# x^T of the second attention 32 bytes further on in its SBUF tile

## The chip, the cores and the metric

The kernel runs on one core of a Trainium2 chip. The metric is the device time of one execution in microseconds (us), as the median of several runs. Engines are named as in the profile: PE (TensorE; PEld is its weight load), DVE (VectorE), ACT (ScalarE), POOL (GpSimd), SP (SyncE, which issues the DMAs).

## What is computed

A decoder trunk of two layers on 256 tokens of 1024 features in float32. Each layer is a mixer and a SwiGLU FFN with RMS norms ahead of both, and a last norm follows. The first mixer is a dilated sliding-window attention with three patterns, the second is forgetting attention. Cut to what matters:

```
h = x
h = h + dilated_mixer(rmsnorm(h, a_norm), a_w_in, a_w_out)
h = h + swiglu(rmsnorm(h, ffn_norm[0]), ffn_w_gu[0], ffn_w_down[0])
h = h + forgetting_mixer(rmsnorm(h, b_norm), b_w_in, b_f, b_w_out)
h = h + swiglu(rmsnorm(h, ffn_norm[1]), ffn_w_gu[1], ffn_w_down[1])
return rmsnorm(h, final_norm)

def forgetting_mixer(h, w_in, b_f, w_out):      # the second attention
    proj = h @ w_in                              # q, k, v of 16 heads, and 16 gates
    log_f = log_sigmoid(gates + b_f); c = cumsum(log_f)
    s = q k^T / 8 + c_i - c_j, causal; p = softmax(s)
    return (p v) @ w_out
```

## The kernel before

There are four stages that read normalised activations as x^T: the first attention, the first FFN, the second attention and the second FFN. In each, x^T lies in one tile "xt" of 128 partitions x 8 (blocks of 128 features) x 2 (high and low part) x 256 tokens, of type fp32r, 16384 bytes per partition. The tag has one buffer, so all four stages use the same addresses. The weights come by DMA in pieces of 128 x 1024 ("raw") and are split by ACT into a high part "wh" and by DVE into a low part "wl" (`piece`, `split`, lines 73 and 75), four buffers of 8192 bytes each.

A product with x^T is three matmuls (`mm3`, lines 178 and 183): high x high, high x low, low x high. It comes in two forms:

- feature products (`proj_feat`): a 128 x 128 block of the weights is stationary, 256 tokens of x^T move, and the result is feature-major. Eight of the second attention's twelve units are of this form (queries and keys of four quads of heads), with 2 x 8 x 3 = 48 matmuls in a unit. The gates and up-projections of the FFNs are of it too.
- token products (`proj_tok`, `proj_pair`): a 128 x 128 block of x^T is stationary and 256 or 512 columns of weights move. The values are made by them, and the first three units of each FFN.

In the profile's rows the moving operand stands first: `ps_mm<-xt,wh` is a feature product, `ps_mm<-wh,xt` a token product. Each matmul has a weight load of its own on PEld, which runs while the matmul before it moves its columns.

Where things lie: the pool "ap" gives each tag a place in the order of first use, in the order h, ot (high and low), gap, xt, xn (the buffers of sums, sqs, junk and xn), rs_a, v, rt, fm0 and so on. The tile "gap" of 112 floats is never read or written; it moves xt. In the built program the weights start at 25952 + n x 8192 bytes, which is 352 modulo 512, and xt at 145184, which is 288 modulo 512: 64 bytes in front of the weights. Blocks of x^T and of the weights follow each other by multiples of 512 bytes, so this holds for every operand of these products, but for those that take every second token. The products of the FFN's way down (`ps_o<-wh,al` and the like) have both operands at 352 modulo 512.

What sets the order around the change: PE runs its matmuls in the order of the code. In the second attention three value units come first, the first two of them together, with the norm of the second 128 tokens (`norm_t`: DVE line 166, PE line 171) between; then the gates (`gates_1`, line 786; `softplus`, the transpose at line 799 and a chain of small steps on DVE and POOL, lines 805 to 818), then the eight feature units and the last value unit. `gates_2` (transposes at 824, a scan at 828, copies at 830) writes the last rows of the key operand "z"; ACT's line 914 writes its other rows. The scores (line 844) of a quad are put between the halves of later feature units, the transposes of the probabilities (275) and the products with v (286) after them. The first scores stand after the first half of the third feature unit.

Line 395 makes "rs_a" with four columns for the first attention's factors of the norm, line 543 "rt" with two columns for the same factors in another order of tokens.

Of the kernel before, what the change touches and what calls it, by code (L numbers as in the profile page):

```python
# [10 lines left out]
F32 = mybir.dt.float32  # L11
F32R = mybir.dt.float32r
AF = mybir.ActivationFunctionType
ALU = mybir.AluOpType
AX = mybir.AxisListType

P = 128
D = 1024
S = 256
KT = D // P  # L20
# [11 lines left out]
def trunk(ctx: ExitStack, tc: tile.TileContext, T, out):  # L32
    nc = tc.nc
# [3 lines left out]
    ap = ctx.enter_context(tc.tile_pool(name="ap", bufs=1))  # L37
# [4 lines left out]
    def first():  # L42

        return tc.high_priority(offset=300)

    def psum(tag):
        return ps.tile([P, 512], F32, tag=tag, name=f"ps_{tag}", bufs=2)
# [15 lines left out]
    mhalf = cst.tile([P, 1], F32, name="mhalf")  # L63
# [30 lines left out]
    def fm_tile(tag, n, bufs):  # L94
        return tuple(ap.tile([P, n, S], F32R, tag=f"{tag}{x}", name=f"{tag}{x}", bufs=bufs) for x in "hl")
# [1 line left out]
    class XT(tuple):  # L97
        pass

    def xt_tile():  # L100
        full = ap.tile([P, KT, 2, S], F32R, tag="xt", name="xt", bufs=1)
        x = XT((full[:, :, 0, :], full[:, :, 1, :]))
        x.full = full
        return x
# [24 lines left out]
    def weights(nm, i, after=None):  # L129

        upto = order.index((nm, i)) + AHEAD
        while state["next"] <= min(upto, len(order) - 1):
            key = order[state["next"]]
            cuts = []
            ready[key] = piece(key, cuts)
            for cut in cuts:
                cut(after)
            state["next"] += 1
        return ready.pop((nm, i))
# [46 lines left out]
    def both(pair, *idx):  # L186
        return tuple(x[idx] for x in pair)


    def early(x, b):  # L190

        x = x.rearrange("p (n b) -> p b n", b=2)
        return x if b is None else x[:, b]
# [58 lines left out]
    def values_12(v, os):  # L252

        for a in range(2):
            v[1 + a] = v_tile()
        with first():
            for t in range(2):
                for a in range(2):
                    rows = slice(a * 64, a * 64 + 64)
                    for g in range(2):  # L260
                        nc.scalar.activation(v[1 + a][g * 64:g * 64 + 64, t * S:(t + 1) * S],
                                             os[t][rows, g * S:(g + 1) * S], AF.Copy, scale=r_a[t][rows])
# [41 lines left out]
    for i, c in enumerate(room):  # L304
        b = 1 + (i > 1)
        n = S + 512
# [12 lines left out]
        for j in range(b):  # L319
            xk.append(both_k[:, j, :S])  # L320
            wk.append(both_k[:, j, S:])

    ap.tile([P, 112], F32, tag="gap", name="gap", bufs=1)
    xt = xt_tile()

    r_a = []
    lead = [psum("sc") for _ in range(2)]
# [62 lines left out]
    def rstd_a():  # L390

        o = psum("tr")
        for t in range(2):
            nc.tensor.matmul(o[:, t:t + 1], part[0][:, t * P:(t + 1) * P], one, start=True, stop=True)
        v = ap.tile([P, 4], F32, tag="rs_a", name="rs_a", bufs=1)
        with first():
            nc.scalar.activation(v[:, :2], o[:, :2], AF.Copy, bias=EPS)
            nc.gpsimd.tensor_tensor(v[:, 2:], v[:, :2], mhalf.to_broadcast([P, 2]), op=ALU.pow)
        r_a.extend(v[:, 2 + t:3 + t] for t in range(2))

    x = []

    ot = fm_tile("ot", KT, 1)
# [99 lines left out]
    for i, (hq, g, w) in enumerate(a_units):  # L503
# [19 lines left out]
        if w < 2:  # L523
# [4 lines left out]
            if i == 2:  # L528
                values_12(quad["v"], lead)

                wt = weights("a_in", 1)
                o_next = psum("mm")
                rb = psum("tr")

                def rows():
                    for t in range(2):
                        nc.tensor.matmul(rb[:, t * P:(t + 1) * P], r_a[t].to_broadcast([P, P]), ident,
                                         start=True, stop=True)

                proj_feat(xt, wt, o_next[:, :S], 0, (6, rows))  # L540
                for c in (rcos, rsin):
                    nc.vector.tensor_tensor(c, c, rb[:, :S], op=ALU.mult)
                rt = ap.tile([P, 2], F32, tag="rt", name="rt", bufs=1)
                tmp = ap.tile([P, D], F32, tag="xn", name="rd", bufs=2)[:, :S].rearrange("p (b c) -> p b c", b=2)
                e = early(rb[:, :S], None)
                nc.vector.tensor_tensor(tmp, e, ident[:, None, :].to_broadcast([P, 2, P]), op=ALU.mult)
                nc.vector.tensor_reduce(rt, tmp, axis=AX.X, op=ALU.add)
# [63 lines left out]
                parts.append(sq(hn[:, s]))  # L611
        return hn, parts

    def out_proj(nm, ot, h, grow, done, banks):

        ws = [weights(nm, i) for i in range(4)]
        xt = xt_tile()
        res = []

        def part(t, acc, nk):  # L620
            last = None
            for n, k in nk:
                c = (k % 2) * D + n * 512
                last = mm3(acc[n], both(ot, ALL, k, slice(t * P, (t + 1) * P)),
                           both(ws[k // 2], ALL, slice(c, c + 512)), k == 0, k == KT - 1)
            return last

        def cols(ks):
            return [(n, k) for n in range(2) for k in ks]

        for t in range(2):
            acc = [psum(banks[t]) for _ in range(2)]
            if t == 0:

                nk = cols(range(done))
                last = part(t, acc, nk[:done])
                nk = nk[done:]
                for i in sorted(due):
                    with tc.issue_after(last.ins):
                        for fn, a in due[i]:  # L640
                            fn(*a)
                    last = part(t, acc, nk[:2]) or last
                    nk = nk[2:]
                due.clear()
                part(t, acc, nk)
                last = part(t, acc, cols(range(done, KT)))
            else:
                part(t, acc, cols(range(2)))
                with tc.issue_after(last.ins):
                    part(t, acc, cols(range(2, 6)))  # L650
                    norm_t(*res[0], grow, xt, 0)
                    part(t, acc, cols(range(6, KT)))
            res.append(residual(acc, h[t], f"h_{nm}{t}"))
        return res, xt
# [93 lines left out]
        return res  # L748

    g_f = load_grow(1)  # L750
    hs, xt = out_proj("a_out", ot, x, g_f, 6, ("sc", "mm"))
    maskb = const("maskb", [P, 3 * P])
    sel = const("sel", [80, NH])
    bf = const("bf", [NH, 1])
    wf32 = const("b_f_in", [P, KT * NH])
    nxt = {}

    def mid(h0):
        nxt["g"] = load_grow(2)
        nxt["xt"] = xt_tile()  # L760
        norm_t(*h0, nxt["g"], nxt["xt"], 0)

    hs = ffn(0, hs, xt, g_f, mid)
    xt, g_b = nxt["xt"], nxt["g"]

# [66 lines left out]
    ot = fm_tile("ot", KT, 1)  # L832
# [99 lines left out]
        for fn, a in due.pop(i, ()):  # L932
            fn(*a)
    g_f = load_grow(3)
    hs, xt = out_proj("b_out", ot, [h for h, _ in hs], g_f, 5, ("mm", "sc"))

    def finish(t, h, parts):
        r = rstd(parts)
# [10 lines left out]
    hs = ffn(1, hs, xt, g_f, mid)  # L949
# [4 lines left out]
    for o, (a, b) in zip(acc, ((0, 512), (512, 256), (768, 256))):  # L954
        s = slice(a, a + b)
# [8 lines left out]
    v = ap.tile([P, 2], F32, tag="rs", name="rs", bufs=4)  # L964
# [99 lines left out]
```

## Time and profile before

| what | us |
|---|---|
| median of 3 runs | 761.44 (761.38 to 761.49) |
| the profiled execution's own time | 761.3 |
| its span, first to last instruction | 759.4 |
| PE busy in the span | 749.7 |
| DVE busy | 511.1 |
| ACT busy | 402.7 |
| POOL busy | 32.4 |

The granted clock of TensorE is 0.997 of full speed over the span. A matmul's duration in the profile is longer than the time from its start to the next one's, since matmuls are pipelined. The distance between starts is what a row of matmuls costs; the mean duration moves with it where nothing is waited for.

### The profile page before, as it was taken

What the parts mean: (1) busy time and instruction counts of PE and PEld (TensorE: products, weight loads), DVE (VectorE), ACT (ScalarE), POOL (GpSimd) and SP (SyncE); (2) the same over time, 40 slices, a digit from 0 to 9 for tenths busy, and PEclk for the clock granted to TensorE, in tenths of its full rate; (3) what the DMA queues carried; (4) which work ended last, traced back from release to release, by engine and by line L of the source; (5) the groups of instructions that cost most, each with busy time, mean ns of one, the idle gap of its engine ahead of it and who ended that gap; (6) DMA issues with size and microseconds to landing.
All of it is one profiled execution on the core that took longest, in us unless ns stands there. A gap on an engine that the chain in (4) does not pass through costs nothing.

```text
span 759.4 us, 14132 instructions
## 1 busy us (share of the span) xinstructions
PE 749.7 (99%) x5810; PEld 695.6 (92%) x5810; DVE 511.1 (67%) x758; ACT 402.7 (53%) x664; POOL 32.4 (4%) x51
## 2 busy tenths in 40 slices
PE   8999999999999999999999999999999999999996
PEld 7999999999998799999999988999889999999995
DVE  6899987986988476555556374888756655556533
ACT  7737539448538455534445354587645434455521
POOL 1110000010010000000000003100000000000000
PEclk9999999999999999999999999999999999999998
DMA  8855553653555367556567444634426665566601
GB/s 329 281 189 192 168 184 105 211 183 104 188 187 177 95 215 243 195 193 195 186 207 239 147 164 142 220 115 142 135 76 228 224 196 193 186 203 202 216 1 55
DMA packets 38352, 135.01 MB, mean 178 GB/s; under 512 B 4368, under 2 KB 5648, under 8 KB 38288
## 3 DMA queue, kind: packets, MB, share of 16 engines
q1 hardware_dynamic: 38144, 134.01, 53.3%
q8 instruction: 45, 0.74, 0.4%
q14 instruction: 19, 0.16, 0.1%
q10 hardware_dynamic: 144, 0.10, 0.0%
HBM read 133.05 MB, written 1.05 MB: 177 GB/s over the span
## 4 chain that ended last, share of the span: by engine, by line
PE 93%; ACT 2%; issue 2%; DMA 1%; DVE 1%; SPq 0%; POOL 0%; POOLq 0%; ACTq 0%; DVEq 0%
PE ps_mm L183 32%; PE ps_mm L178 17%; PE ps_tr L183 9%; PE ps_sc L183 9%; PE ps_o L183 7%; PE ps_tr L178 5%; PE ps_sc L178 4%; PE ps_o L178 3%; PE ps_tr L275 2%; PE ps_o L286 2%; PE ps_sc L844 1%; DMA otl<-in_lead 1%; ACT wh L73 1%; PE ps_tr L171 1%; PE ps_sc L441 1%
## 5 line engine op out<-in xcount | busy, mean ns | idle before, releaser
L73 ACT ACTIVATE wh<-raw 128x1024 fp32r<-128x1024 f32 x236 | 244.0, 1056 | 220.0 <-PE ps_tr L183 67.3
L75 DVE TENSOR_TENSOR wl<-raw,wh 128x1024 fp32r<-128x1024 f32 x236 | 284.6, 1222 | 99.1 <-ACT wh L73 98.7
L178 PE MATMUL ps_mm<-xt,wh 128*128 128x256 f32 x816 | 227.2, 279 | 0.0
L183 PE MATMUL ps_mm<-xt,wl 128*128 128x256 f32 x816 | 225.8, 277 | 0.1
L183 PE MATMUL ps_mm<-xt,wh 128*128 128x256 f32 x816 | 225.7, 277 | 0.0
L178 PEld LDWEIGHTS ps_mm<-xt,wh 128*128 128x128 f32 x816 | 153.3, 188 | 0.6 <-issue 0.3
L183 PEld LDWEIGHTS ps_mm<-xt,wl 128*128 128x128 f32 x816 | 153.3, 188 | 0.5 <-DVE wl L75 0.5
L183 PEld LDWEIGHTS ps_mm<-xt,wh 128*128 128x128 f32 x816 | 153.4, 188 | 0.1
L183 PE MATMUL ps_tr<-xt,wh 128*128 128x256 f32 x304 | 83.8, 276 | 0.0
L183 PE MATMUL ps_tr<-xt,wl 128*128 128x256 f32 x304 | 83.8, 276 | 0.0
L178 PE MATMUL ps_tr<-xt,wh 128*128 128x256 f32 x304 | 83.6, 276 | 0.0
L685 DVE TENSOR_TENSOR sa<-ps_tr,sa 128x256 f32<-128x256 f32 x38 | 16.1, 424 | 73.6 <-PE ps_tr L183 73.6
L183 PEld LDWEIGHTS ps_tr<-xt,wh 128*128 128x128 f32 x304 | 57.1, 188 | 0.0
L183 PEld LDWEIGHTS ps_tr<-xt,wl 128*128 128x128 f32 x304 | 57.1, 188 | 0.0
L178 PEld LDWEIGHTS ps_tr<-xt,wh 128*128 128x128 f32 x304 | 56.9, 188 | 0.0
L178 PE MATMUL ps_mm<-wh,xt 128*128 128x256 f32 (+1 forms) x160 | 53.1, 332 | 0.0
L183 PE MATMUL ps_mm<-wl,xt 128*128 128x256 f32 (+1 forms) x164 | 52.2, 322 | 0.0
L183 PE MATMUL ps_mm<-wh,xt 128*128 128x256 f32 (+1 forms) x164 | 52.1, 321 | 0.0
L183 PEld LDWEIGHTS ps_mm<-wl,xt 128*128 128x128 f32 x164 | 31.1, 190 | 2.6
L183 PEld LDWEIGHTS ps_mm<-wh,xt 128*128 128x128 f32 x164 | 30.8, 190 | 2.8 <-DVE xt L75 0.3
L178 PEld LDWEIGHTS ps_mm<-wh,xt 128*128 128x128 f32 x160 | 30.4, 190 | 3.0
L183 PE MATMUL ps_sc<-wh,al 128*128 128x512 f32 (+1 forms) x82 | 31.4, 387 | 0.0
(237 smaller groups left out, 1170.3 us busy)
## 6 DMA issues: line engine op xcount, KB each, us to landing
raw<-in_gu SPq DMA_DIRECT2D x88, 512.0 KB, 4.7
raw<-in_a_in SPq DMA_DIRECT2D x68, 512.0 KB, 4.3
raw<-in_dn SPq DMA_DIRECT2D x44, 512.0 KB, 4.7
raw<-in_b_in SPq DMA_DIRECT2D x24, 512.0 KB, 4.8
raw<-in_a_out SPq DMA_DIRECT2D x8, 512.0 KB, 5.3
raw<-in_b_out SPq DMA_DIRECT2D x8, 512.0 KB, 3.9
grow<-in_norms SPq DMA_DIRECT2D x4, 512.0 KB, 6.1
x<-in_x SPq DMA_DIRECT2D x2, 512.0 KB, 5.4
```

The costliest lines, as they stand in the source:

```text
L73: a = nc.scalar.activation(view(hi), src, AF.Copy)
L75: return a, nc.vector.tensor_tensor(view(lo), src, view(hi).bitcast(F32), op=ALU.subtract)
L171: nc.tensor.transpose(tr[:, k * P:(k + 1) * P], xn[:, kk * P:(kk + 1) * P], ident)
L178: nc.tensor.matmul(o, sh, mh, start=start, stop=False)
L183: last = nc.tensor.matmul(o[:, u], s, m[:, u], start=False, stop=end and u.stop == n)
L275: nc.tensor.transpose(tr[:, i * P:(i + 1) * P], b, ident)
L286: nc.tensor.matmul(o[h * HD:(h + 1) * HD], v[:, c:c + HD], w(h), start=start, stop=stop)
L441: nc.tensor.matmul(sc[h][a * 64:a * 64 + 64, o:o + 64], q[hr[h], b // 2, c], k[hr[h], b // 2, c], start=True, stop=True)
L685: nc.vector.tensor_tensor(a, u, sg, op=ALU.mult)
L844: last = nc.tensor.matmul(scs[h][:, qb * P:qb * P + (qb + 1) * P], qz[h][rows[h], pr, qb * P:(qb + 1) * P], kz[h][rows[h], pr, :(qb + 1) * ...
```

## The change

`xt_tile` gets an argument "front", the distance in bytes at which x^T lies in front of the weights modulo 512. The tile is made 120 floats longer than x^T, and x^T starts 128 - front/4 floats into it. The first attention and both FFNs ask for 64, the second attention for 32. The tile "gap" goes, and the two columns of "rt" become columns 4 and 5 of "rs_a", which grows from four to eight.

In the built program the tile starts at 144736, where "gap" was. x^T of three stages stays at 145184. That of the second attention is at 145216, which is 320 modulo 512. The tiles between xt and rt (the two xn buffers, rs_a, the seven v buffers) lie 32 bytes higher than before, v at 352 instead of 320 modulo 512. From fm0 on every tile has its old address, and so has everything in front of xt. The instructions of every engine, their order and their waits are the same as before.

```diff
-    def xt_tile():
-        full = ap.tile([P, KT, 2, S], F32R, tag="xt", name="xt", bufs=1)
+    def xt_tile(front):
+        n = KT * 2 * S
+        at = 128 - front // 4
+        tile = ap.tile([P, n + 120], F32R, tag="xt", name="xt", bufs=1)[:, at:at + n]
+        full = tile.rearrange("p (k x s) -> p k x s", k=KT, x=2)
         x = XT((full[:, :, 0, :], full[:, :, 1, :]))
...
-    ap.tile([P, 112], F32, tag="gap", name="gap", bufs=1)
-    xt = xt_tile()
+    xt = xt_tile(64)
...
-        v = ap.tile([P, 4], F32, tag="rs_a", name="rs_a", bufs=1)
+        v = ap.tile([P, 8], F32, tag="rs_a", name="rs_a", bufs=1)
...
+        r_a.append(v[:, 4:6])
...
-                rt = ap.tile([P, 2], F32, tag="rt", name="rt", bufs=1)
+                rt = r_a.pop()
...
-    def out_proj(nm, ot, h, grow, done, banks):
+    def out_proj(nm, ot, h, grow, done, banks, front):
...
-        xt = xt_tile()
+        xt = xt_tile(front)
...
-        nxt["xt"] = xt_tile()
+        nxt["xt"] = xt_tile(32)
```

Both calls of `out_proj`, which make the x^T of the two FFNs, pass 64.

## Rows read from the trace of the kernel before

**Rows 1.** The profile page: the span, the engines' busy time, and the chain that ended last by engine.
```profile
span 759.4 us, 14132 instructions
...
PE 749.7 (99%) x5810; PEld 695.6 (92%) x5810; DVE 511.1 (67%) x758; ACT 402.7 (53%) x664; POOL 32.4 (4%) x51
...
PE 93%; ACT 2%; issue 2%; DMA 1%; DVE 1%; SPq 0%; POOL 0%; POOLq 0%; ACTq 0%; DVEq 0%
```

**Rows 2.** Windows: stretch in us, its length, busy time (and instructions) of each engine, granted clock, DMA share, GB/s. First attention, then the second attention in two stretches of feature units.
```profile
14.00:240.00 226.00, 225.89 (x2041) 213.65 (x2040) 198.87 (x304) 134.23 (x221) 11.16 (x17) 1.00 0.56 185
...
472.10:498.00 25.90, 25.66 (x212) 25.21 (x211) 19.15 (x44) 17.32 (x36) 4.54 (x3) 1.00 0.48 164
498.00:532.20 34.20, 34.20 (x287) 31.41 (x286) 28.31 (x58) 25.62 (x62) 2.51 (x4) 1.00 0.46 146
```

**Rows 3.** Timeline of PE (start in us, duration in us, what): the first matmul of a feature unit and that of the next one, in the first attention and in the second.
```profile
29.55 0.28 PE L178 MATMUL ps_mm<-xt,wh 128*128 128x256 f32 x1
...
34.99 0.28 PE L178 MATMUL ps_mm<-xt,wh 128*128 128x256 f32 x1
...
472.11 0.28 PE L178 MATMUL ps_mm<-xt,wh 128*128 128x256 f32 x1
...
477.76 0.28 PE L178 MATMUL ps_mm<-xt,wh 128*128 128x256 f32 x1
```

**Rows 4.** Groups of PE's instructions by line and shape from 14 to 240 us (first attention), feature products: count, busy us, mean ns of one, idle before.
```profile
L183 PE MATMUL ps_mm<-xt,wl 128*128 128x256 f32 x384 | 106.3, 277 | 0.1
L183 PE MATMUL ps_mm<-xt,wh 128*128 128x256 f32 x384 | 106.1, 276 | 0.0
```

**Rows 5.** The same from 472 to 498 us (second attention).
```profile
L183 PE MATMUL ps_mm<-xt,wl 128*128 128x256 f32 x64 | 18.0, 281 | 0.0
L183 PE MATMUL ps_mm<-xt,wh 128*128 128x256 f32 x64 | 18.0, 281 | 0.0
```

**Rows 6.** The same from 498 to 543 us (second attention; 192 feature products up to 532 us).
```profile
L183 PE MATMUL ps_mm<-xt,wh 128*128 128x256 f32 x65 | 18.0, 277 | 0.0
L183 PE MATMUL ps_mm<-xt,wl 128*128 128x256 f32 x65 | 18.0, 276 | 0.0
```

**Rows 7.** The same from 262 to 450 us (first FFN): feature products, then products of the way down with both operands at the same place modulo 512, of 512 and of 256 columns.
```profile
L183 PE MATMUL ps_tr<-xt,wl 128*128 128x256 f32 x152 | 41.9, 276 | 0.0
...
L183 PE MATMUL ps_o<-wl,ah 128*128 128x512 f32 x30 | 11.7, 389 | 0.0
...
L183 PE MATMUL ps_o<-wh,al 128*128 128x256 f32 x16 | 3.2, 283 | 0.0
...
L183 PE MATMUL ps_o<-wl,ah 128*128 128x256 f32 x16 | 3.2, 280 | 0.0
```

**Rows 8.** The same from 450 to 472 us (second attention), token products of 512 and 256 columns. L178's mean holds the first one after a transpose.
```profile
L183 PE MATMUL ps_mm<-wh,xt 128*128 128x512 f32 x15 | 6.0, 400 | 0.0
L183 PE MATMUL ps_mm<-wl,xt 128*128 128x512 f32 x15 | 5.9, 395 | 0.0
...
L183 PE MATMUL ps_sc<-wh,xt 128*128 128x256 f32 x16 | 4.5, 280 | 0.0
L183 PE MATMUL ps_sc<-wl,xt 128*128 128x256 f32 x16 | 4.5, 279 | 0.0
```

**Rows 9.** The chain that ended last, from 482 to 488 us: start, us, what.
```profile
486.62 0.24 issue
486.86 1.33 PE ps_sc L844 x7
```

**Rows 10.** Timeline of DVE around the gates, 469 to 487 us; in brackets the idle time before and what ended it.
```profile
469.29 0.19 DVE L805 COPY gates<-ps_tr 128x32 f32<-128x32 f32 x1 [0.26 <-PE ps_tr L799]
...
475.46 0.18 DVE L810 TENSOR_SCALAR gates<-gates 128x32 f32<-128x32 f32 x1 [5.54 <-POOL gates L809]
...
482.70 2.36 DVE L75 TENSOR_TENSOR wl<-raw,wh 128x1024 fp32r<-128x1024 f32 x2
484.98 0.67 DVE L828 TENSOR_TENSOR_SCAN v<-v,ps_tr 16x256 f32<-16x256 f32 x1
485.69 0.86 DVE L830 COPY z<-v 16x512 f32<-16x512 f32 x2
```

**Rows 11.** Timeline of ACT at the same place.
```profile
485.08 1.06 ACT L73 ACTIVATE wh<-raw 128x1024 fp32r<-128x1024 f32 x1 [2.50 <-DVE wl L75]
486.17 1.21 ACT L914 ACTIVATE z<-ps_mm 64x512 f32<-64x512 f32 x2
```

**Rows 12.** Timeline of PE from 498.6 us: the first feature products after transposes.
```profile
498.82 0.28 PE L183 MATMUL ps_mm<-xt,wh 128*128 128x256 f32 x1
498.94 0.28 PE L183 MATMUL ps_mm<-xt,wl 128*128 128x256 f32 x1
499.06 0.28 PE L178 MATMUL ps_mm<-xt,wh 128*128 128x256 f32 x1
499.17 0.28 PE L183 MATMUL ps_mm<-xt,wh 128*128 128x256 f32 x1
499.29 0.28 PE L183 MATMUL ps_mm<-xt,wl 128*128 128x256 f32 x1
```

**Rows 13.** Timeline of DVE at the second norm, and at the weight split ahead of the gates' sums.
```profile
457.37 1.42 DVE L166 SCALAR_TENSOR_TENSOR xn<-hf,rs,grow 128x512 f32<-128x512 f32 x2 [0.46 <-POOL rs L151]
...
465.56 2.36 DVE L75 TENSOR_TENSOR wl<-raw,wh 128x1024 fp32r<-128x1024 f32 x2 [4.60 <-ACT wh L73]
```

**Rows 14.** Groups of PE's instructions from 14 to 240 us: products of the probabilities with v, 64 columns.
```profile
L286 PE MATMUL ps_o<-pt,v 128*64 128x64 f32 x96 | 3.8, 221 | 0.0
```

More of the change, by code (lines that the diff above doesn't have):

```diff
@@ L394, in rstd_a @@
             nc.tensor.matmul(o[:, t:t + 1], part[0][:, t * P:(t + 1) * P], one, start=True, stop=True)
-        v = ap.tile([P, 4], F32, tag="rs_a", name="rs_a", bufs=1)
+        v = ap.tile([P, 8], F32, tag="rs_a", name="rs_a", bufs=1)
         with first():
             nc.scalar.activation(v[:, :2], o[:, :2], AF.Copy, bias=EPS)
-            nc.gpsimd.tensor_tensor(v[:, 2:], v[:, :2], mhalf.to_broadcast([P, 2]), op=ALU.pow)
+            nc.gpsimd.tensor_tensor(v[:, 2:4], v[:, :2], mhalf.to_broadcast([P, 2]), op=ALU.pow)
         r_a.extend(v[:, 2 + t:3 + t] for t in range(2))
+        r_a.append(v[:, 4:6])
     x = []
@@ L750, in trunk @@
     g_f = load_grow(1)
-    hs, xt = out_proj("a_out", ot, x, g_f, 6, ("sc", "mm"))
+    hs, xt = out_proj("a_out", ot, x, g_f, 6, ("sc", "mm"), 64)
     maskb = const("maskb", [P, 3 * P])
@@ L934, in trunk @@
     g_f = load_grow(3)
-    hs, xt = out_proj("b_out", ot, [h for h, _ in hs], g_f, 5, ("mm", "sc"))
+    hs, xt = out_proj("b_out", ot, [h for h, _ in hs], g_f, 5, ("mm", "sc"), 64)
     def finish(t, h, parts):
```

## Prediction

> **What bounds the kernel now.** The page comes first: PE is busy for 749.7 of the 759.4 us of the span, and the chain that ended last is PE for 93% [rows 1]. The windows by stage then say that PE has no gap worth the name in the stages concerned, and that the granted clock is 1.00 in all of them [rows 2]. So a time is won or lost here by how fast PE goes through its matmuls, unless PE is made to wait for something that another engine delivers at a time of its own.
>
> What is to be seen next is that matmuls of one shape don't all go at one pace. I take the pace from starts in the timeline: in the first attention 48 feature products (x^T moving, 256 columns) start at 29.55 and the next 48 at 34.99 us, which is 5.44 / 48 = 113.3 ns each; in the second attention 48 of the same take from 472.11 to 477.76 us, 5.65 / 48 = 117.7 ns [rows 3]. The mean duration of one tells the same in whole nanoseconds, 276 against 281, and is quicker to read over long stretches: 276 for the first attention [rows 4], 281 for the second from 472 to 498 us [rows 5], 276 again for it from 498 to 532 us [rows 6], 276 in the first FFN [rows 7]. So before the change one half of the second attention's feature products goes at the long pace, the other half at the short one, at the very same addresses.
>
> Other relative addresses have paces too. Where x^T is stationary (64 bytes in front of the moving weights) a 256-column product takes 279 or 280 ns [rows 8]. Where both operands are at the same place modulo 512 (the halved products of the FFN's way down) it takes 280 and 283 [rows 7]. 276 is the least and 283 the most that a settled 256-column product shows, so these two are my bounds for any product with x^T at the new place.
>
> **The change part by part.** No instruction is added, taken away or moved, and no wait or semaphore differs; the code moves addresses alone. There are three parts.
>
> 1. x^T of the second attention, 64 to 32 bytes in front of the weights. The products that read it: 8 feature units of 48, so 384 (192 of them at the long pace, 192 at the short one); 96 token products of 256 columns with x^T stationary; some 50 token products of 512 columns; 8 for the gates.
>
> *Feature products, long half (472 to 498 us).* If the new place settles them at the short pace they win 192 x (117.7 - 113.3) = 0.85 us of PE work; if at the worst that a row shows they lose 192 x 2 ns (281 to 283) = 0.38 us. But not all of this is on the path. The chain shows PE stopped for 0.24 us in front of the first scores at 486.86 us [rows 9]. What it waits for is no matmul. Scores need the operand z. Its last pieces are DVE's copies from 485.69 us (0.86 us) and ScalarE's at 486.17 us, which stand behind a weight split that waited 2.50 us for DVE [rows 10, 11]. DVE works without a break since 475.46 us, and there it had idled 5.54 us for a POOL instruction that follows the gates' transpose at 469 us [rows 10]. So from the gates' transpose on there is a chain over POOL, DVE and ScalarE whose length doesn't depend on PE's pace. The 48 + 48 + 24 = 120 feature products ahead of the first scores would win 0.53 us and hand all of it back as a longer wait: 0.24 + 0.53 = 0.77 us. What stays are the 24 + 48 = 72 products from 488 to 498 us: 72 x 4.4 = 0.32 us. After 488 us PE waits for nothing in this stage: 0.24 us is all the idle time of its first half, and the second has none [rows 2]. So these 0.32 us go through to the end, past the output projection and the FFN, where PE is just as full. On the losing side the wait is a cover of 0.24 us and then gone.
>
> *Feature products, short half (498 to 532 us).* Nothing to win. Bounds: 0, and 192 x 7 ns (276 to 283) = 1.34 us lost. I take 0: they enter from transposes and settle within a few steps (the starts from 498.82 to 499.06 us lie 0.12 us apart, the next one 0.11 [rows 12]; over all of them the means are 277 and 276 [rows 6]), so the short pace is one they are drawn to, and 32 bytes are half of the distance to the place where 283 is seen.
>
> *Token products (x^T stationary).* At 280 now; bounds 276 and 283, so from -4 to +3 ns each. 24 of the 96 are at 469 to 472 us, inside the stretch that the gates' chain covers. The others are 18 that follow the norm's transposes at 459.32 us, the 6 ahead of them, and 48 of the last value unit at 532 to 543 us. 72 x (-4 to +3) is -0.29 to +0.22 us. I take 0, since the new distance (32) lies between one with 280 (64) and one with 280 and 283 (0).
>
> *Wide token products.* 395 and 400 ns [rows 8] against 389 at equal places [rows 7]: at best 50 x 8 = 0.4 us. More than half stands ahead of 457.37 us, where the second norm on DVE sets the time of the transposes [rows 13], or beside the weight split that DVE begins at 465.56 us and that the gates' sums are queued behind [rows 13]; I count 0.1 us at most on the path, and take 0.
>
> 2. The tiles behind x^T (xn with its users, rs_a, v) lie 32 bytes higher. v is the stationary operand of the products with the probabilities: 64-column ones take 221 ns in the first attention [rows 14], and they come in pairs that overlap. 256 of them in all; 1 ns each way is 0.26 us, and I take 0. They could alter the pace at which the next feature products settle, see the rivals.
>
> 3. rt is now a piece of rs_a. Same writer, same readers, same waits: 0.
>
> The sum is -0.32 us on the profiled execution, whose own time is 761.3 us (span 759.4), 0.14 under the median of 761.44. I apply it to the median: 761.1 us.
>
> What speaks against a change of any size is a rule of the Trainium skill, TensorE: Matmul & The Clock Gate, Part 2, step by step: PE has two independent read ports, one for the moving operand and one for the weight load, so loading the next weights takes no bandwidth from the running matmul. By it the place of one operand against the other could not matter and the sum would be 0 (761.4). The trace bears it out in part only: it has 276, 280 and 283 ns for one shape at different places, which the rule has no cause for, but it also has 276 and 281 at one and the same place.
>
> **The rivals.**
> *The place does nothing; how PE enters decides.* For it: the long half is entered from token products at 280 and then from scores, the short half from transposes, and the addresses are the same in both [rows 5, 6]. Against it: the token products stand at 279 and 280 in all three of their rows, though some of them follow transposes and others wide products [rows 8]. Then the 72 products stay at 117.7 and the time is 761.4.
>
> *The long pace everywhere.* At 32 bytes the short pace is no longer settled on and the other 192 feature products go at 281 too: 192 x 4.4 = +0.85 us, 762.3 us. For it: the long pace exists at 64 already, and stays for 48 products and more in a row. Still within the bound of no change.
>
> *The pace of equal places, the slower side.* 32 bytes may be near enough to 0 that the 283 ns of [rows 7] hold. Short half +1.34; the 72 exposed ones of the long half 72 x 2 = +0.14; token products +0.22; the 144 covered steps 120 x 2 + 24 x 3 = 0.31, less the cover of 0.24, +0.07. That is +1.77 us, 763.2 us. It decides from 113.3 + 4 ns in the short half on, since 0.2% (what a measurement of this kernel can tell from no change) is 1.52 us and the short half brings most of it.
>
> *The tiles moved along.* v or xn at a new place lets feature units elsewhere settle otherwise. A unit of 48 that goes from the short pace to the long one costs 48 x 4.4 = 0.21 us, and one that settles wrongly can hand its pace on to the next. Four units: +0.85 us beside the -0.32, so 762.0 us. Hardly any gain is to be had there, as the rows already say 276 [rows 4].
>
> **How the numbers follow.** Forecast (long half to the short pace, 120 steps of it lost to the gates' chain): 761.1 us, 0.43. No effect: 761.4, 0.24. Long pace everywhere: 762.3, 0.14. Pace of equal places: 763.2, 0.11. Tiles moved along: 762.0, 0.08. The low end is the forecast with token and wide products at their best, 761.12 - 0.29 - 0.1 = 760.7, less 0.2 us for what entries may bring: 760.5. The high end takes in the long pace everywhere with token products at their worst, 762.3 + 0.22, so 762.6; the pace of equal places is left out. Faster than 759.92 is reached by no case, 0.02 for what I have not seen; slower than 762.96 by most of the pace of equal places, 0.09; 0.89 in between.
>
> **What would show it.** In the profile after: the feature products of 472 to 498 us at 276 ns instead of 281, those of 498 to 532 us still at 276; PE's stop in front of the first scores (L844, a line that moves by four) grown from 0.24 to about 0.8 us; token products of the second attention near 280; all rows of the other stages as they were. The forecast is wrong if the stop stays at 0.24 us while the products are faster (then the chain over DVE is no anchor and 0.5 us more are won), if 281 or more stands at 498 to 532 us, or if the first attention's or an FFN's groups change at all.

## The result and the profile after

| what | before | after |
|---|---|---|
| median of 5 runs, us | 761.49 (761.38 to 762.82) | 764.41 (764.01 to 765.19) |
| ratio | | 1.0041, 95% interval 1.0030 to 1.0051 |
| the profiled execution's own time, us | 761.3 | 765.19 |
| its span, us | 759.4 | 763.2 |

The change makes the kernel 2.9 us (0.4%) slower. The forecast was 761.1 us and its range ended at 762.6. The profiled execution of after is the slowest of its five runs, so its 3.8 us of longer span are some 0.9 us more than the medians differ by.

The page of after answers to [rows 1]. The whole difference of the spans is PE's: 753.5 - 749.7 = 3.8 us more busy time with the same 5810 matmuls, and the chain that ended last is as much PE's as before.

```profile
span 763.2 us, 14132 instructions
...
PE 753.5 (99%) x5810; PEld 699.2 (92%) x5810; DVE 510.4 (67%) x758; ACT 402.1 (53%) x664; POOL 32.9 (4%) x51
...
PE 93%; ACT 2%; issue 2%; DMA 1%; DVE 1%; SPq 0%; POOL 0%; POOLq 0%; ACTq 0%; DVEq 0%
```

Where along the span does it arise? The timeline of PE at the places of [rows 3] (start in us, duration, what) tells it by subtraction.

```profile
29.87 0.28 PE L183 MATMUL ps_mm<-xt,wh 128*128 128x256 f32 x1
...
35.52 0.28 PE L183 MATMUL ps_mm<-xt,wh 128*128 128x256 f32 x1
...
474.80 0.28 PE L183 MATMUL ps_mm<-xt,wh 128*128 128x256 f32 x1
...
480.48 0.28 PE L183 MATMUL ps_mm<-xt,wh 128*128 128x256 f32 x1
```

At the unit that began at 29.55 us before, after is 0.32 us late; at the first feature unit of the second attention (472.11 before) it is 2.69 us late. The first products that read the moved x^T are token products, ahead of that unit: they start at 451.90 us before and at 454.54 us after, so after is 2.64 us late there already. So 2.32 of the 3.8 us are lost between 29.55 us and any product that reads the moved x^T. The unit at 29.87 us takes 5.65 / 48 = 117.7 ns a product, where it took 113.3. The rest, 3.8 - 2.69 = 1.1 us, is lost behind 472 us.

The groups by stage put names to it. First attention (14 to 240 us), to be held against [rows 4]: the feature products went from 277 and 276 to 279.

```profile
L188 PE MATMUL ps_mm<-xt,wl 128*128 128x256 f32 x384 | 107.2, 279 | 0.1
L188 PE MATMUL ps_mm<-xt,wh 128*128 128x256 f32 x384 | 107.0, 279 | 0.0
```

A mean of 279 is not one pace, but a mixture. The same view of after from 30 to 46 us, a stretch of feature products alone, has 281:

```profile
L188 PE MATMUL ps_mm<-xt,wl 128*128 128x256 f32 x46 | 12.9, 281 | 0.0
L183 PE MATMUL ps_mm<-xt,wh 128*128 128x256 f32 x46 | 12.9, 281 | 0.0
```

and the windows say the same without durations. They are given for three stretches, first of before, then of after (columns as in [rows 2]): PE has no gap in any, the granted clock is 1.00 in all, and after gets 138 matmuls into 16 us where before got 144, 214 where it got 225, 213 where it got 227.

```profile
30.00:46.00 16.00, 16.00 (x144) 16.00 (x143) 15.65 (x26) 9.43 (x12) 0.00 (x0) 1.00 0.64 217
...
119.00:143.00 24.00, 24.00 (x225) 23.66 (x224) 19.13 (x32) 19.56 (x37) 0.00 (x0) 1.00 0.39 128
...
179.00:205.00 26.00, 26.00 (x227) 25.88 (x226) 20.24 (x31) 18.78 (x26) 0.00 (x0) 1.00 0.44 142
```

```profile
30.00:46.00 16.00, 16.00 (x138) 16.00 (x137) 14.90 (x24) 9.52 (x12) 0.00 (x0) 1.00 0.61 202
...
119.00:143.00 24.00, 24.00 (x214) 23.50 (x213) 19.17 (x33) 20.42 (x39) 0.00 (x0) 1.00 0.36 118
...
179.00:205.00 26.00, 26.00 (x213) 25.55 (x212) 19.77 (x32) 19.08 (x30) 0.00 (x0) 1.00 0.45 143
```

The first FFN (262 to 450 us, answering to [rows 7]) is as it was:

```profile
L188 PE MATMUL ps_tr<-xt,wl 128*128 128x256 f32 x152 | 41.9, 276 | 0.0
```

Second attention, 472 to 498 us (answering to [rows 5]) and 498 to 543 us (to [rows 6]): the long half stayed at 281, the short half went from 277 and 276 to 281.

```profile
L188 PE MATMUL ps_mm<-xt,wh 128*128 128x256 f32 x56 | 15.7, 281 | 0.0
L188 PE MATMUL ps_mm<-xt,wl 128*128 128x256 f32 x56 | 15.7, 281 | 0.0
```

```profile
L188 PE MATMUL ps_mm<-xt,wl 128*128 128x256 f32 x73 | 20.5, 281 | 0.0
L188 PE MATMUL ps_mm<-xt,wh 128*128 128x256 f32 x73 | 20.5, 281 | 0.0
```

PE's stop in front of the first scores (chain that ended last, answering to [rows 9]) is 0.36 us, not the 0.8 that was forecast: the products ahead of it did not become faster.

```profile
489.37 0.36 issue
489.73 1.33 PE ps_sc L848 x7
```

### The profile page after: what moved, and what is told of

Read it like the earlier page. It is cut to its first block, busy times and chain, and to the rows that moved or that the text cites. A ratio compares the mean times of both kernels' runs of the same rounds, so it can differ in the third digit from the quotient of the medians.

```text
span 763.2 us, 14132 instructions
## 1 busy us (share of the span) xinstructions
PE 753.5 (99%) x5810; PEld 699.2 (92%) x5810; DVE 510.4 (67%) x758; ACT 402.1 (53%) x664; POOL 32.9 (4%) x51
## 4 chain that ended last, share of the span: by engine, by line
PE 93%; ACT 2%; issue 2%; DMA 1%; DVE 1%; SPq 0%; POOL 0%; POOLq 0%; ACTq 0%; DVEq 0%
PE ps_mm L188 33%; PE ps_mm L183 17%; PE ps_tr L188 9%; PE ps_sc L188 9%; PE ps_o L188 7%; PE ps_tr L183 5%; PE ps_sc L183 4%; PE ps_o L183 3%; PE ps_tr L280 2%; PE ps_o L291 2%; PE ps_sc L848 1%; DMA otl<-in_lead 1%; ACT wh L73 1%; PE ps_tr L176 1%; PE ps_sc L445 1%
## 5 line engine op out<-in xcount | busy, mean ns | idle before, releaser
L183 PE MATMUL ps_sc<-wh,ah 128*128 128x512 f32 x80 | 31.4, 392 | 0.0
```

The source lines that it names most:

```text
L183: nc.tensor.matmul(o, sh, mh, start=start, stop=False)
```

## The experiments

Two numbers go through this section. Both are counted from the starts in PE's timeline of one profiled execution of each kernel: how many feature products were followed by the next matmul after 115.5 to 125 ns (called long; the short pace is 113.3), and by how much the steps of all feature products of a stage exceed 113.33 ns (called excess; steps over 125 ns hold a change of shape or a wait and are left out). Before has 66 long ones of 1152 in the first attention (excess 0.37 us) and 197 of 384 in the second (0.90 us); after has 591 (2.71 us) and 356 (1.84 us). The two FFNs have some 25 long ones of 912 each (0.18 us) in every kernel but the two that move their x^T.

The theories that the expectations name: **A**, two causes: the tiles moved along (v, xn) change the pace on which stretches of the first attention settle, and x^T at 32 has no short pace. **B**, chance: a stretch settles on either pace from one execution to the next, whatever the addresses. **C**, the moved tiles make the whole loss. **D**, what counts of v is its place against the tile "pt" that moves over it in the products with the probabilities. **E**, what counts of v is its place against the operands of the feature products that follow.

**The parts of the change, one by one.** First the moved tiles without x^T at 32: after, with one number altered.

```diff
-        nxt["xt"] = xt_tile(32)
+        nxt["xt"] = xt_tile(64)
```

> x^T of the second attention back at 64 bytes; xn, rs_a and v stay 32 bytes higher, as after the change. Theory A (two causes: the new place of x^T costs about 1.1 us in the second attention, the tiles moved along cost the first attention what is left): about 763.3 us, feature products of the second attention from its second half on at 276 ns again, stretches of the first attention at 281. Theory B (the place of x^T is the one cause, the first attention goes at the long pace by chance in some executions of any version): the median of before, 761.5 us, with single executions up to 2 us above. Theory C (the moved tiles alone make the whole loss, in both attentions): 764.4 us.

Measured: 764.05 us (763.62 to 764.2) against 761.11 (760.04 to 762.69) for before on the same chip, ratio 1.0039 (1.0025 to 1.0053). Long products: 602 in the first attention, 83 in the second. Groups from 14 to 240 us:

```profile
L183 PE MATMUL ps_mm<-xt,wh 128*128 128x256 f32 x384 | 107.6, 280 | 0.0
L188 PE MATMUL ps_mm<-xt,wl 128*128 128x256 f32 x384 | 107.2, 279 | 0.1
```

So the loss in the first attention comes from the tiles alone, and it is most of what the whole change costs. By its time alone this kernel lies nearer to theory C's 764.4 us than to A's 763.3; what tells them apart are the groups, the next kernel and the repeats further down. The second attention did in part what the prediction had hoped to get from x^T at 32: the 120 products ahead of the first scores went short but for 5, though x^T did not move, while of the 72 behind the scores 70 stayed long. And the stop in front of the first scores grew to 0.73 us:

```profile
489.07 0.46 PE L848 MATMUL ps_sc<-z,z 80*128 80x128 f32 x2 [0.73 <-ACT z L918]
```

Then the reverse: x^T of the second attention at 32, and every tile behind it 512 bytes on, so that their places modulo 512 stay. Three small tiles of the second attention share the buffers of the first one's for the room.

```diff
-        full = ap.tile([P, KT, 2, S], F32R, tag="xt", name="xt", bufs=1)
+        n = KT * 2 * S
+        tile = ap.tile([P, n + 128], F32R, tag="xt", name="xt", bufs=1)[:, at:at + n]
...
-        nxt["xt"] = xt_tile()
+        nxt["xt"] = xt_tile(8)
...
-        nm = stat_tile("nm_b", 4)
+        nm = stat_tile("nm", 4)
```

> Only x^T of the second attention is 32 bytes in front of the weights; every other tile keeps its old place modulo 512 (those behind x^T lie 512 bytes higher, and the second attention's small statistics share the first one's buffers). Theory A: about 762.6 us, all feature products of the second attention at 281 ns or so, the first attention at 276. Theory B: 764.4 us or, in executions without the chance, 762.6. Theory C: 761.5 us.

Measured: 761.82 us (761.26 to 762.71), ratio 1.0011 (1.0002 to 1.0019). The first attention has 63 long products, as before; the second 354 of 384. Groups from 498 to 543 us:

```profile
L185 PE MATMUL ps_mm<-xt,wl 128*128 128x256 f32 x64 | 18.0, 281 | 0.0
L185 PE MATMUL ps_mm<-xt,wh 128*128 128x256 f32 x64 | 18.0, 281 | 0.0
```

In front of the first scores PE no longer stops at all (the product ahead starts at 485.99, the scores at 486.27 us). x^T at 32 is a loss by itself, of 0.7 us (A had put it at 1.1), and it doesn't touch the first attention.

**Which of the moved tiles.** v alone, 32 bytes on behind a pad; then xn alone, by placing rs_a ahead of it.

```diff
-        v = ap.tile([P, 4], F32, tag="rs_a", name="rs_a", bufs=1)
+        v = ap.tile([P, 8], F32, tag="rs_a", name="rs_a", bufs=1)
+        ap.tile([P, 8], F32, tag="pad", name="pad", bufs=1)
...
-                rt = ap.tile([P, 2], F32, tag="rt", name="rt", bufs=1)
+                rt = r_a.pop()
```

> Only v is 32 bytes higher than before (352 modulo 512); x^T, xn and rs_a are at their old places. If v is what the first attention's loss hangs on (its products with the probabilities stand right in front of feature units that changed pace), 762.5 to 763.5 us with stretches of the first attention at 281 ns. If it hangs on xn or rs_a, or on chance, 761.5 us.

```diff
+    rs = ap.tile([P, 4], F32, tag="rs_a", name="rs_a", bufs=1)
     sums = ap.tile([P, D], F32, tag="xn", name="sums", bufs=2)
...
-        v = ap.tile([P, 4], F32, tag="rs_a", name="rs_a", bufs=1)
+        v = rs
```

> Only xn (with sums, sqs, junk) is 32 bytes higher than before; x^T, rs_a and v are at their old places modulo 512. If the first attention's loss hangs on xn (the sums are the first stationary operand after a feature unit at 22 us), 762.5 us or more with the stretch from 26 to 46 us at 281 ns. Otherwise 761.5 us.

In the second kernel rs_a lies in front of the two xn buffers, 8192 bytes lower. That is a multiple of 512, so modulo 512 only xn has moved.

Measured: v alone 762.80 us (761.91 to 763.72), ratio 1.0021 (1.0012 to 1.0030); xn alone 761.63 us (760.82 to 762.72), ratio 1.0007 (0.9998 to 1.0016), not to be told from no change. Its expectation had 762.5 us or more if the stretch from 26 us went to 281: the stretch did, and the time stayed below. But the groups divide cleanly. One row each from 30 to 46 us and from 123 to 143 us, first of v alone, then of xn alone:

```profile
L183 PE MATMUL ps_mm<-xt,wl 128*128 128x256 f32 x48 | 13.2, 276 | 0.0
...
L183 PE MATMUL ps_mm<-xt,wl 128*128 128x256 f32 x55 | 15.5, 281 | 0.0
```

```profile
L183 PE MATMUL ps_mm<-xt,wl 128*128 128x256 f32 x46 | 12.9, 281 | 0.0
...
L183 PE MATMUL ps_mm<-xt,wl 128*128 128x256 f32 x57 | 15.7, 276 | 0.0
```

The stretches at 22 and 26 us go with xn, those from 121 us on with v. The table has the long products of each stretch that changed (its start in before, and how many products it has). Its last column is a kernel of the next step.

| stretch | what stands ahead on PE | before | after | tiles | v | xn | v and pt |
|---|---|---|---|---|---|---|---|
| 22 us, 30 | norm's sums | 28 | 2 | 1 | 29 | 2 | 27 |
| 26 us, 174 | transposes with rs_a | 1 | 173 | 173 | 1 | 173 | 1 |
| 121 us, 144 | products with v | 2 | 142 | 142 | 142 | 2 | 3 |
| 138 us, 48 | transposes of probabilities | 2 | 47 | 47 | 47 | 2 | 47 |
| 180 us, 144 | token products | 2 | 144 | 144 | 144 | 2 | 144 |
| 197 us, 48 | transposes of probabilities | 2 | 47 | 47 | 47 | 2 | 47 |

Stretches are of one pace or the other, from end to end. The five further kernels that leave v and xn of the first attention in place (x^T alone, twice; gates' sums; two with x^T at other distances) have the paces of before in all six stretches, and those that move both have the paces of after (one exception is told below). Theory B falls by that for these six. Chance is not gone altogether: the first stretch of all, 36 products at 17 us, has 4 to 8 long ones in before and in four of those five, and 23 in the fifth; and 24 products at 488 us, right behind the first scores, have 23 long ones in the profile of the tiles alone above and 4 in a second profile of the same kernel. The other stretches of the first attention have 2 to 4 long products in every kernel.

At 26 us the entry already tells the paces apart. Behind the transposes of rs_a the steps of before are 206, 119, 113, 113 ns, those of after 200, 119, 117, 118, 118 (from the starts in ns; the timeline prints them to 10 ns). The first step is 206 or 207 ns in all eight profiles in which the stretch begins at the short pace and 200 or 201 in all five in which it begins at the long one.

**What of v it is.** In the first attention v is the stationary operand beside pt, in the second the tag holds the sums of the gates. So pt was moved by the same 32 bytes as v (which leaves their distance; on top of the kernel with v alone, and with one buffer less of a small tag for the room). In another kernel nothing but the gates' sums was moved, to a buffer of another tag.

```diff
+            moved.append(ap.tile([P, 8], F32, tag="pad2", name="pad2", bufs=1))
         w = ap.tile([P, 512], F32, tag="pt", name="pt", bufs=3)
```

> As the kernel in which only v is 32 bytes higher, but pt, the moving operand of the products with v, is moved by the same 32 bytes, so that the two stand to each other as before. Theory D (what counts is where the two operands of the products in front stand to each other): the stretches from 121 to 143 us and from 180 to 202 us are back at 276 ns, about 761.5 us. Theory E (what counts is where v stands to the operands of the feature products that follow): they stay at 281 ns, 762.8 us.

```diff
-    gt = v_tile()
+    gt = ap.tile([P, 512], F32, tag="qr", name="gt", bufs=3)
```

> Only the tile of the gates' sums (one of the v buffers in the second attention) lies 32 bytes higher modulo 512; all v proper and x^T are as before. Theory: the entry behind the gates' transpose sets the pace of the two feature units from 472 us on, as it did where all of v was moved, so these go at 276 ns; the first scores still come about 17.7 us after the gates' transpose, so PE hands the 0.53 us back as a longer stop: the same time as before within 0.3 us. Rival (the stop shrinks along): 0.5 us less than before.

Measured, v and pt: one run of 762.22 us, against 761.29 (760.65 to 762.26). The stretch behind the products with v is short again (last column of the table), and the other three are not. Theory D agrees with the one stretch that directly follows products of pt with v, and is wrong for the rest; theory E is wrong for that one and not refuted for the rest. A kernel with pt alone moved was not run, so that pt's own place does it is not excluded.

Measured, gates' sums: 761.24 us (760.85 to 763.04), ratio 1.0001 (0.9992 to 1.0010). The 120 products ahead of the first scores became short but for 6 (118 of them were long before), 0.5 us of excess less; the 72 behind stayed long but for 2. None of the gain is in the time: the stop in front of the first scores took it.

```profile
486.54 0.35 PE L844 MATMUL ps_sc<-z,z 80*128 80x128 f32 x1 [0.69 <-ACT z L914]
```

0.24 us in [rows 9], 0.69 here. This is the clean test of the chain over POOL, DVE and ACT that the prediction built on, as nothing else is altered. One pair of stops would be thin evidence, since the stop is 0.00 to 0.36 us in the eight profiles with long products ahead of it. It is 0.40 to 1.00 us in the five with short ones (0.73 and 0.49 in the two profiles of the tiles alone), 0.5 us more in the mean, while the time from the gates' transpose to the first scores is the same in both groups: 17.5 to 18.0 and 17.5 to 18.1 us.

**Is there a better place than 64 or 32?** Three stages at another distance each, the first attention at 64; other tiles at their old places modulo 512, with the same three small tiles sharing buffers.

```diff
-    hs, xt = out_proj("a_out", ot, x, g_f, 6, ("sc", "mm"))
+    hs, xt = out_proj("a_out", ot, x, g_f, 6, ("sc", "mm"), 96)
...
-        nxt["xt"] = xt_tile()
+        nxt["xt"] = xt_tile(128)
...
-    hs, xt = out_proj("b_out", ot, [h for h, _ in hs], g_f, 5, ("mm", "sc"))
+    hs, xt = out_proj("b_out", ot, [h for h, _ in hs], g_f, 5, ("mm", "sc"), 32)
```

> x^T of the first FFN 96 bytes in front of the weights, of the second attention 128, of the second FFN 32; the first attention at 64 and all other tiles at their old places modulo 512. Theory A says that at 32 the long pace is the only one: the second FFN's 912 feature products go at 280 ns or more and that stage takes 912 x 5 ns = 4.5 us longer. The rival (the long pace at 32 belongs to the second attention's entries alone) leaves the second FFN at 276. For 96 and 128 there is no forecast from a row; 276 to 283 ns each, so between 0 and +6 us for the first FFN, -0.5 to +2.5 us for the second attention.

The other kernel has 192, 256 and 160 there.

> The same with 192 bytes for the first FFN, 256 for the second attention and 160 for the second FFN. No forecast from a row: 276 to 283 ns for the feature products, 276 to 283 for the token products of 256 columns. If some place has both at 276, a version with all stages there would win some 4 ns on each of 400 token products, 1.5 us and more.

Measured: 769.97 and 772.89 us, one run each, against 761.29. Groups, each with one row of the first FFN (262 to 450 us), the second attention (472 to 498 us) and the second FFN (590 to 740 us): 96, 128, 32 and then 192, 256, 160.

```profile
L186 PE MATMUL ps_mm<-xt,wl 128*128 128x256 f32 x152 | 42.5, 280 | 0.0
...
L186 PE MATMUL ps_mm<-xt,wl 128*128 128x256 f32 x54 | 15.2, 281 | 0.0
...
L186 PE MATMUL ps_mm<-xt,wl 128*128 128x256 f32 x149 | 41.8, 281 | 0.0
```

```profile
L186 PE MATMUL ps_mm<-xt,wl 128*128 128x256 f32 x152 | 42.4, 279 | 0.0
...
L186 PE MATMUL ps_mm<-xt,wl 128*128 128x256 f32 x52 | 14.7, 283 | 0.0
...
L186 PE MATMUL ps_mm<-xt,wl 128*128 128x256 f32 x141 | 39.8, 282 | 0.0
```

By steps the feature products take 117.4 ns at 96, 118.6 at 128, 118.4 at 32, 117.8 at 192, 119.8 at 256 and 120.0 at 160, in the mean of each stage, against 113.5 at 64. The times follow: the excess of the three stages is 3.69 + 1.97 + 4.58 us in the first kernel, and less the 0.18 + 0.90 + 0.18 us of before that is 9.0 us (measured 8.7); 4.10 + 2.44 + 6.09 less the same are 11.4 us in the second (11.6). At 32 the second FFN is long throughout, 877 of 912 products, as theory A said. Of the seven distances tried 64 is the only one with a short pace, so for the second attention no better place was found. Each distance but 32 was tried in one stage and one execution, and the weights stood at one place in all of them: whether the distance counts or x^T's own place modulo 512 is not separated.

**Do the parts add?** The first comparison had left 2.94 us for the tiles, 0.71 for x^T and 2.92 for both, on different chips. So all three were run once more, on one chip and against the same runs of before.

> The whole change, taken again on the same chip and in the same runs as its two parts. If the two parts add (moved tiles +2.9 us, x^T at 32 +0.7 us), the whole stands at +3.2 to +3.6 us over before; the whole is then at least 0.3 us slower than the moved tiles alone. If they don't add (what x^T at 32 loses is given up inside the stretch that the gates' chain covers, or is lost only where the moved gates' sums would have won), it stands within 0.3 us of the moved tiles alone.

> The moved tiles without x^T at 32, beside the whole change. Both theories: 762.8 to 764.2 us, +2.3 to +3.0 over before, if the long pace of some 520 feature products in the first attention at 4.4 ns each is the cause. If this time it stands within 1 us of before, the first comparison was chance.

> x^T at 32 with every other tile at its old address in front of fm0, beside the whole change. By the paces +0.94 us of PE work, of which about 0.3 us fall in front of the first scores: +0.6 to +0.9 us over before. If the parts add, this is what the whole change has over the moved tiles alone.

Measured against 761.24 us (760.35 to 762.83):

| kernel | us | ratio |
|---|---|---|
| whole change | 764.75 (763.84 to 765.08) | 1.0043 (1.0029 to 1.0057) |
| tiles only | 763.32 (762.46 to 764.24) | 1.0027 (1.0018 to 1.0036) |
| x^T only | 762.19 (761.57 to 763.68) | 1.0013 (1.0004 to 1.0022) |

2.08 + 0.95 = 3.03 us for the parts, 3.51 for the whole: they add within what the intervals allow, and the whole stands 1.43 us over the tiles alone. Theory C, already shaken by x^T alone, is out. The sizes were forecast less well: the whole lies in its 3.2 to 3.6 us, the tiles alone lie below their 2.3 to 3.0 and x^T alone a little above its 0.6 to 0.9.

The whole change's second profile has one thing that its first one had not: in the long stretch at 26 us PE stopped for 0.41 us, and after the stop the products went at the short pace. By the view it waited at the first product of a unit for DVE's reading of an earlier unit's result (fm, line 416), which DVE began at 29.42 us, behind a weight split, and in the first profile at 28.66 us. The timeline of PE:

```profile
29.57 0.28 PE L188 MATMUL ps_mm<-xt,wl 128*128 128x256 f32 x1
30.26 0.36 PE L183 MATMUL ps_mm<-xt,wh 128*128 128x256 f32 x1 [0.41 <-DVE fm L416]
30.45 0.28 PE L188 MATMUL ps_mm<-xt,wh 128*128 128x256 f32 x1
30.57 0.28 PE L188 MATMUL ps_mm<-xt,wl 128*128 128x256 f32 x1
30.68 0.28 PE L183 MATMUL ps_mm<-xt,wh 128*128 128x256 f32 x1
30.80 0.28 PE L188 MATMUL ps_mm<-xt,wh 128*128 128x256 f32 x1
30.91 0.28 PE L188 MATMUL ps_mm<-xt,wl 128*128 128x256 f32 x1
31.02 0.28 PE L183 MATMUL ps_mm<-xt,wh 128*128 128x256 f32 x1
```

30 of that stretch's 174 products are long there instead of 173. So a stretch kept its pace until a stop in its middle, and such a stop differs from run to run. It is one case. Another stop of the same profile, 0.37 us in front of the transposes with rs_a, changed neither the first step behind them (200 ns) nor the pace.

**The ledger.** For each kernel the excess in the two attentions less that of before, and beside it the time. A gain in the second attention is counted as nothing, since it lies ahead of the first scores (but for 0.08 us of it in two rows) and the stop there takes it; a loss is counted in full.

| kernel | first attention, us | second attention, us | sum by that rule | measured, us |
|---|---|---|---|---|
| whole change | +2.34 | +0.94 | 3.3 | +2.92 |
| whole change again | +1.70 | +0.93 | 2.6 | +3.51 |
| tiles only | +2.38 | -0.50 | 2.4 | +2.94 |
| tiles only again | +2.39 | -0.57 | 2.4 | +2.08 |
| x^T only | 0.00 | +0.95 | 1.0 | +0.71 |
| x^T only again | +0.01 | +0.95 | 1.0 | +0.95 |
| v | +1.73 | -0.50 | 1.7 | +1.69 |
| xn | +0.68 | 0.00 | 0.7 | +0.52 |
| v and pt | +1.04 | -0.58 | 1.0 | +0.93 (one run) |
| gates' sums | +0.01 | -0.50 | 0.0 | -0.05 |

The rule holds within 0.6 us in all rows but one, in a kernel whose executions of one and the same program lie up to 2.7 us apart (760.04 to 762.69). The row that is off by 0.9 us, the whole change again, is the one whose profiled run had the stop of 0.41 us, and the other of 0.37 us in front of the transposes with rs_a; with the two it comes to 3.4 us. Whether its other runs had them too is not known.

The profiles' own times agree with the first column. From the first feature product of the first attention to that of the first FFN before takes 275.76 us. The whole change takes 2.32 us more, the tiles 2.35 and 2.41, v 1.68, xn 0.68, v and pt 1.08, the gates' sums 0.06 less; the whole change again 2.97 more, with its two stops. x^T alone takes 0.66 and 0.03 us less.

None of the versions is faster than before. The gates' sums alone have the least excess in the two attentions (0.78 us against 1.27), and PE's busy time (749.8 against 749.7 us) and the time of before.

## Why the prediction was wrong

**It failed at step 2, the tiles moved along.** The prediction put v and xn at 0 in its sum, where the runs showed 2.3 us, and kept "v or xn at a new place lets feature units elsewhere settle otherwise" as a rival at 0.08, with four units of 0.21 us. The mechanism of that rival is what happens, and its size was too small: 591 - 66 = 525 products, eleven units, go from the short to the long pace, 2.3 us. The number of units at risk could have been counted instead of guessed: the trace of before shows 66 long products of 1152 there, so 1086 could turn, and 1086 x 4.4 ns = 4.8 us was the bound on the losing side. It would have put the measured time inside the range. Two of the prediction's own signs of being wrong came true: 281 at 498 to 532 us, and a changed group in the first attention.

**Step 1, short half: the rival "long pace everywhere" was right.** The forecast reasoned that 32 lies half way between 64 and equal places, and that a stretch which settles at 64 is "drawn to" the short pace. x^T alone at 32 shows 354 of 384 products long, +0.95 us of excess: 0.86 in the short half for the forecast's 0 (the rival had 0.85), 0.09 in the long one. The half-way argument had no row behind it: the paces of 96, 128 and 192 are not ordered by distance either.

**Step 1, long half.** At 32 it did not become short: 281 stays. In the kernels that left x^T at 64 the part ahead of the first scores could be made short by moving the gates' sums. Of the 72 products behind the scores, whose 0.32 us were the whole of the forecast's gain, 70 stayed long in three of these profiles. In two, the second one of the tiles alone and that of v and pt, 24 became short but for 4 and the other 48 stayed long but for 1. So a short pace behind the scores does occur at 64, and what brings it was not found.

**The cover was right.** That a faster first half is handed back as a longer stop in front of the first scores is shown by the gates' sums alone (0.24 to 0.69 us, time unchanged) and agrees with the tiles alone (0.73 and 0.49 us) and with v alone (0.40). It is also why the tiles' gain of 0.5 us in the second attention does not offset their loss in the first.

**Token and wide products** are where they were put: 279 ns for x^T at 32 in after, and 402 and 394 for the wide ones that had 400 and 395. One reading was off: [rows 8] shows two rows of 256 columns, at 280 and 279, while the third in that view (L178) has 291. Nothing was found for the 64-column products with v themselves (221 ns in both, [rows 14]); it is what follows them that changes.

**The rule that was weighed**, TensorE: Matmul & The Clock Gate, Part 2 of the Trainium skill, says nothing there of an operand's byte offset in SBUF; read as the prediction read it, it gives 0 for any change of place, and the runs are against that reading: matmuls of the same shape go at 113.5 ns at 64 and at 118.4 to 120.0 at 32, 160 and 256. What it says of loads that take nothing from running matmuls may still hold; the runs don't show by what the place matters.

**Two sums of the prediction don't come out**, and neither bears on the result. The rival of equal places "decides" not from 4 ns in the short half on but from (1.52 - 0.14 - 0.22 - 0.07) / 192 = 5.7 ns, and the high end, 762.3 + 0.22, is 762.5.

**What stays open.** Why a stretch falls to one pace is not settled. Shown is that places of operands ahead of it decide (32 bytes modulo 512 of xn, of v, of the gates' sums), that at 26 us the first step already differs (206 or 200 ns), and that one stop in the middle of a stretch ended its pace. The stretches at 138, 180 and 197 us go with v but not with the distance from v to pt, and what of v they depend on was not found. That a difference of some 5 ns in when the first product starts picks the pace is a guess that fits the entry at 26 us; at 138 and 197 us the first step is 200 to 202 ns at either pace. The table leaves room for another reading of the stretch at 26 us: it begins long exactly where the one ahead of it is short. xn stands in the norm's sums ahead of that earlier stretch, so whether it acts on the stretch at 26 us by itself or by way of the one at 22 us was not separated.

## What to carry to other kernels

A shift of one buffer by a few bytes is an edit of every tile behind it, and an operand's place can change the pace of matmuls that don't read it: when one tile is moved, pad behind it so that the others keep their places modulo 512, and compare the mean durations of all stages, not of the one that was meant. Where PE is full and has two paces for one shape, count the stretches that could change pace and put their whole price into the range: here no row of before said which would. And before trying to win pace in a stretch, look which wait stands at its end: 0.5 us of faster matmuls were worth nothing in front of scores that waited for ACT.

## What was not expected of the hardware

- Feature products of 256 columns at one address have two paces, 113.3 and 117.7 ns, and keep either for up to 174 products at a granted clock of 1.00; in one profile a stop of 0.41 us ended the long one.
- A move by 32 bytes modulo 512 of a tile that the products don't read (xn, v, or the gates' sums) turns stretches of 30 to 174 products from one pace to the other, the same ones in every kernel that moves that tile, but for one of v's four when pt was moved with it.
- With x^T the moving operand, 64 bytes in front of the weights modulo 512 is the only distance of seven (32, 64, 96, 128, 160, 192, 256) that has the short pace; the others take 117.4 to 120.0 ns in the mean. The weights' own place was the same in all. At 192 the token products are a little faster than at 64 (278 against 280 ns in the first FFN), and the feature products slower.
